# The second block's attention: GpSimd's large operations to VectorE, keys unpadded in pairs, scores in one pool of banks

## The chip, the cores and the metric

The kernel runs on one core of a Trainium2 chip. The metric is the device time of one execution in microseconds (us); lower is better. TensorE multiplies matrices into PSUM, VectorE, ScalarE and GpSimd work elementwise, and the queue of SyncE issues the loads.

## What is computed

Two transformer blocks over 256 tokens of width 1024, in float32. The first (two layers of retention, sliding-window and latent attention with a mixture of experts) is untouched. The second is a hybrid mixer, a projection with residual, and an MLP:

```python
proj = h @ w_in                                   # q, k, v, xl, gl: 512 columns each
q = rms_norm_2(q per head, q_norm_g); k = rms_norm_2(k per head, k_norm_g)
attn = stick_breaking_attention(q, k, v)          # 8 heads of 64
lru = rg_lru(causal_depthwise_conv(xl)) * gelu(gl)
x = x + concatenate([attn, lru]) @ w_out
x = x + square(relu(rms_norm_2(x) @ w_up)) @ w_down
```

and for each head of the attention, with z = q k^T / 8 and the mask kpos < qpos:

```python
log_one_minus = where(mask, log_sigmoid(-z), 0)
suffix = reverse_cumsum(log_one_minus) - log_one_minus
w = where(mask, exp(log_sigmoid(z) + suffix), 0);  out = w @ v
```

## The kernel before

Weights come from HBM in units of 128x1024 float32 (512 KB) into tiles `u`, in the order of use, as many ahead as there are buffers. Each unit is split into two float32r parts: a high half, which ScalarE casts (`unit_hi`, L247), and a low half, the unit minus its high half (`unit_lo`, L251, one subtract of 1024 columns). Every product of a weight is then three matmuls (`mm3`, L377 to L379: high by high, high by low, low by high). `both_halves` makes both parts of a unit ahead of its use on an engine that it names; `unit` does so where that has not happened.

The changed part is `mix_second`. Its first half stands in a block of manual order, so there ScalarE, VectorE and GpSimd run their instructions as they are written: k's RMS scaling (`Normed`: the sums of squares `sums`, the power -0.5 on GpSimd in `roots` and `rpow` at L365, the scaling `apply` at L1471, the transposes `turn` at L1477), the gates and the scan of the recurrent branch (L1535), then the same for q, with the low halves of the q and gl units between. GpSimd makes the low halves of gl units 1 and 3. After that, in `gelu` and in the loop over heads, a list scheduler orders the instructions; `high_priority` puts the heads' steps first.

Keys are laid out twice (`kz`): in one tile the even heads with zeros in the upper 64 rows, in the other the odd heads with zeros in the lower 64, so that each score product contracts 128 rows. For each head, `head` (L1565 on) makes the transposed scores z of 384 columns (the 256 queries against the first 128 keys, and the last 128 queries against the last 128 keys; L1569 and L1570), adds the mask by a product with the identity (L1571, L1572), and forms softplus(z) as max(z, 0) + ln(1 + exp(-|z|)): Abs, Exp and Ln on ScalarE (L1574, L1576, L1577), max and add on VectorE (L1578). `head_w` subtracts the running sums by triangular products into the same bank (L1582 to L1584) and takes the exponential (L1586). `weighted_v` multiplies the weights of two heads with the values, one into the lower and one into the upper 64 partitions (L487, L489), and splits the result. Heads run two ahead of their weights (`DEEP = 2`). The scores of even heads lie in banks of the pool psA, of odd heads in psB (`ZB = "AB"`); each pool has four banks, and psB also takes the results of `weighted_v` and the transposes. psA takes the projections' accumulators too: gl's two, and the four of the output projection.

`gelu` (called at head 1) makes the gate of the recurrent branch: a product on GpSimd (L1550), three operations of 1024 columns on VectorE (L1551 to L1553), Exp, Ln, Exp on ScalarE, and the product L1559 in two halves. The output projection `out_proj` needs four accumulators in psA; its units 0 to 3 take the recurrent branch, 4 to 7 the heads. The low halves of its units 0, 2, 4 and 6 are GpSimd's:

```python
POOL_LO = {("wo", 2): (0, 2, 4, 6)}
ZB = "AB"
```

Of the kernel before, what the change touches and what calls it, by code (L numbers as in the profile page):

```python
# [19 lines left out]
P = 128  # L20
S = 256
# [10 lines left out]
NU, NV, NH = 29, 20, 8  # L32
POOL_LO = {("wo", 2): (0, 2, 4, 6)}
HP = 100
DEEP = 2
ZB = "AB"
TAIL = 5
# [77 lines left out]
def tile_hybrid(ctx: ExitStack, tc: tile.TileContext, A, out, taps=None):  # L115
# [137 lines left out]
    def unit(name):  # L253

        if name not in ready:
            unit_hi(name)
            unit_lo(name, POOL if name[0] in POOL_LO and name[1] in POOL_LO[name[0]] else DVE)
        _, hi, lo = ready.pop(name)
        return [(hi[:, j, :], lo[:, j, :]) for j in range(hi.shape[1])]
# [187 lines left out]

    BLK = (slice(0, 128), slice(128, 384))

    def softmax_p(s, scale, sink):  # L450
# [943 lines left out]
    def mix_second(hT, params, scale, vp):  # L1394
# [50 lines left out]
        qT = st([P, 4, S], F32, "v")  # L1445
        kz = [st([P, 4, S], F32, "v") for _ in range(2)]
        POOL.memset(kz[0][64:128], 0.0)
        POOL.memset(kz[1][0:64], 0.0)

        class Normed:  # L1450
# [12 lines left out]
            def roots(self, i):  # L1463
                s8 = self.s8[i]
                POOL.tensor_scalar(s8[:, 1], s8[:, 0], scale[i][:, 3:4], RMS_EPS, op0=OP.mult, op1=OP.add)
                rpow(s8[:, 2], s8[:, 1])
                POOL.tensor_scalar(s8[:, 2], s8[:, 2], scale[i][:, 2:3], None, op0=OP.mult)

            def apply(self, i):
                self.qn[i] = qn = st([P, 512], F32, "h")  # L1470
                DVE.tensor_tensor(qn.rearrange("p (h e) -> p h e", h=8), self.ps[i].rearrange("p (h e) -> p h e", h=8),  # L1471
                                  self.s8[i][:, 2, :, None].to_broadcast([P, 8, 64]), op=OP.mult)

            def turn(self, i):
                ps = bank("B")
                for b in range(4):
                    PE.transpose(ps[:, b * P:(b + 1) * P], self.qn[i][:, b * P:(b + 1) * P], ident)  # L1477
                pb = ps.rearrange("p (b t) -> p b t", b=4)
                t = slice(i * P, (i + 1) * P)
                if self.name == "q":  # L1480
                    ACT.activation(qT[:, :, t], pb, AF.Copy, scale=qg[:, 0:1])
                else:
                    for b in range(2):
                        r = slice(64 * b, 64 * b + 64)
                        DVE.tensor_scalar(kz[b][r, :, t], pb[r], qg[r, 1:2], None, op0=OP.mult)

# [8 lines left out]
        with tc.manual_schedule(engines={ACT.engine, DVE.engine, POOL.engine}):  # L1495
# [21 lines left out]
            def turn_k(u):  # L1517
                if u == 3:
                    kk.turn(0)
                    both_halves("gl", 0, DVE)  # L1520
                    kk.turn(1)
                    both_halves("gl", 1, POOL)

# [12 lines left out]
            for i in range(2):  # L1536
                qq.apply(i)
            both_halves("gl", 3, POOL)

# [7 lines left out]
        def gelu():  # L1547

            ge = st([P, 4, S], F32, "v")
            POOL.tensor_tensor(u_, u_, gx, op=OP.mult)  # L1550
            DVE.scalar_tensor_tensor(ge, gx, 0.044715, gx, op0=OP.mult, op1=OP.mult)  # L1551
            DVE.scalar_tensor_tensor(ge, ge, 1.0, gx, op0=OP.add, op1=OP.mult)
            DVE.tensor_scalar(ge, ge, -27.0, None, op0=OP.max)  # L1553
            with tc.issue_after(both.ins):
                ACT.activation(ge, ge, AF.Exp, scale=-2.0 * math.sqrt(2.0 / math.pi))
            ACT.activation(ge, ge, AF.Ln, bias=1.0)
            ACT.activation(ge, ge, AF.Exp, scale=-1.0)
            for c in (slice(0, 2), slice(2, 4)):
                DVE.tensor_tensor(aa[:, c], ge[:, c], u_[:, c], op=OP.mult)  # L1559
                split_out(mt[1][0][:, c], mt[1][1][:, c], aa[:, c])  # L1560
            tap("lru", [m[0].bitcast(F32) for m in mix[4:8]])
# [3 lines left out]

        def head(h):
            f, kk = h // 2, kz[h % 2][:, h // 2, :]
            z = bank(ZB[h % len(ZB)])
            PE.matmul(z[:, 0:S], kk[:, 0:P], qT[:, f, :], start=True, stop=False, **kw)  # L1569
            PE.matmul(z[:, S:384], kk[:, P:S], qT[:, f, P:S], start=False, stop=False, **kw)  # L1570
            PE.matmul(z[:, 0:P], identB, masks["m_stick"], start=False, stop=False, **kw)  # L1571
            PE.matmul(z[:, S:384], identB, masks["m_stick"], start=False, stop=True, **kw)  # L1572
            ab = st([P, 384], F32, "h")
            ACT.activation(ab, z[:, :384], AF.Abs)  # L1574
            with tc.issue_after(both.ins):
                ACT.activation(ab, ab, AF.Exp, scale=-1.0)  # L1576
            ACT.activation(ab, ab, AF.Ln, bias=1.0)  # L1577
            DVE.scalar_tensor_tensor(ab, z[:, :384], 0.0, ab, op0=OP.max, op1=OP.add)  # L1578
            return z, ab
# [8 lines left out]

        zs, ws = [], []
        for n in range(8 + DEEP):  # L1590
            if n < 8:
                with tc.high_priority(HP):
                    zs.append(head(n))
            if n == GELU:
# [169 lines left out]
```

## Time and profile before

| | us |
|---|---|
| median of three runs | 808.78 (807.9 to 810.78) |
| the profiled execution, its own time | 816.43 |
| its span, first to last instruction | 814.6 |
| TensorE busy | 776.5 (95%) |
| VectorE busy | 460.0 (56%) |
| ScalarE busy | 337.6 (41%) |
| GpSimd busy | 137.9 (17%) |

The page's shares are means over the whole kernel. The second block's heads and gelu lie between about 577 and 607 us, the output projection from 607 to 630, the MLP from 630 to the end. "PEclk" is the clock granted to TensorE as a share of full speed (2.4 GHz; a half is 1.2). In a timeline, the brackets behind a row give how long the engine had been idle before it and which instruction let it go on. Consecutive rows of one engine can overlap: a record ends when the result is written, and the next instruction starts earlier.

### The profile page before, as it was taken

What the parts mean: (1) busy time and instruction counts of PE and PEld (TensorE: products, weight loads), DVE (VectorE), ACT (ScalarE), POOL (GpSimd) and SP (SyncE); (2) the same over time, 40 slices, a digit from 0 to 9 for tenths busy, and PEclk for the clock granted to TensorE, in tenths of its full rate; (3) what the DMA queues carried; (4) which work ended last, traced back from release to release, by engine and by line L of the source; (5) the groups of instructions that cost most, each with busy time, mean ns of one, the idle gap of its engine ahead of it and who ended that gap; (6) DMA issues with size and microseconds to landing.
All of it is one profiled execution on the core that took longest, in us unless ns stands there. A gap on an engine that the chain in (4) does not pass through costs nothing. (4 is left out here: it accounts for less than half of the span.)

```text
span 814.6 us, 13248 instructions
## 1 busy us (share of the span) xinstructions
PE 776.5 (95%) x5098; PEld 556.8 (68%) x5098; DVE 460.0 (56%) x834; ACT 337.6 (41%) x611; POOL 137.9 (17%) x176
## 2 busy tenths in 40 slices
PE   6999899999999999999899998899879999999998
PEld 4997678443324897778443333598758999999997
DVE  4697745632227688855723216677856655555722
ACT  4566522321213566631311113438764644544710
POOL 1400222260002310102236002114910000000000
PEclk9999999999999999999999999999999999999999
DMA  8992097899999763086899999664403565666101
GB/s 315 407 355 82 1 361 296 304 403 364 411 353 342 280 216 130 27 330 231 306 357 385 407 354 384 213 201 133 139 40 125 185 202 186 199 187 186 50 1 51
DMA packets 57666, 193.45 MB, mean 237 GB/s; under 512 B 8960, under 2 KB 9856, under 8 KB 57600
## 3 DMA queue, kind: packets, MB, share of 16 engines
q1 hardware_dynamic: 57600, 192.57, 65.0%
q8 instruction: 41, 0.67, 0.3%
q14 instruction: 25, 0.20, 0.1%
HBM read 191.50 MB, written 1.05 MB: 236 GB/s over the span
## 5 line engine op out<-in xcount | busy, mean ns | idle before, releaser
L251 DVE TENSOR_TENSOR u<-u,u 128x1024 fp32r<-128x1024 f32 (+5 forms) x151 | 180.6, 1212 | 67.8 <-ACT u L247 41.7
L247 ACT CAST u<-u 128x1024 fp32r<-128x1024 f32 (+4 forms) x159 | 158.1, 1015 | 93.6 <-DVE u L251 44.5
L377 PE MATMUL psA<-u,v 128*128 128x512 f32 (+1 forms) x272 | 111.1, 409 | 6.0 <-ACT u L247 6.0
L1019 PE MATMUL psB<-u,v 128*32 128x512 f32 x864 | 113.9, 602 | 1.9 <-PEq L1143 1.2
L378 PE MATMUL psA<-u,v 128*128 128x512 f32 (+1 forms) x272 | 107.9, 397 | 0.8 <-DVE u L251 0.8
L379 PE MATMUL psA<-u,v 128*128 128x512 f32 (+1 forms) x272 | 107.3, 395 | 0.0
L379 PE MATMUL psB<-v,u 128*128 128x256 f32 x256 | 72.4, 283 | 0.0
L378 PE MATMUL psB<-v,u 128*128 128x256 f32 x256 | 72.3, 283 | 0.0
L377 PE MATMUL psB<-v,u 128*128 128x256 f32 x256 | 72.3, 284 | 0.0
L1019 PEld LDWEIGHTS psB<-u,v 128*32 128x32 f32 x864 | 29.7, 111 | 61.0 <-issue 54.5
L377 PEld LDWEIGHTS psA<-u,v 128*128 128x128 f32 x272 | 52.8, 194 | 16.4 <-ACT u L247 6.5
L1079 PE MATMUL psB<-u,h 128*32 128x512 f32 x496 | 62.7, 594 | 0.8 <-DMA u<-in_exp_w_down_dram 0.8
L378 PEld LDWEIGHTS psA<-u,v 128*128 128x128 f32 x272 | 52.5, 193 | 11.8 <-issue 1.7
L379 PEld LDWEIGHTS psA<-u,v 128*128 128x128 f32 x272 | 52.8, 194 | 10.4 <-issue 0.8
L369 DVE TENSOR_TENSOR h<-psB,h 128x512 fp32r<-128x512 f32 x30 | 20.8, 692 | 59.0 <-ACT h L368 59.0
L377 PE MATMUL psA<-u,h 128*128 128x512 f32 (+1 forms) x136 | 53.0, 390 | 0.0
L378 PE MATMUL psA<-u,h 128*128 128x512 f32 (+1 forms) x136 | 52.7, 387 | 0.0
L379 PE MATMUL psA<-u,h 128*128 128x512 f32 (+1 forms) x136 | 52.0, 386 | 0.0
L378 PEld LDWEIGHTS psB<-v,u 128*128 128x128 f32 x256 | 49.1, 192 | 0.5
L377 PEld LDWEIGHTS psB<-v,u 128*128 128x128 f32 x256 | 48.9, 192 | 0.7 <-ACT v L368 0.2
L379 PEld LDWEIGHTS psB<-v,u 128*128 128x128 f32 x256 | 49.1, 192 | 0.0
L379 PE MATMUL psA<-v,u 128*128 128x256 f32 (+1 forms) x170 | 48.0, 283 | 0.7 <-POOL u L251 0.7
(345 smaller groups left out, 1327.5 us busy)
## 6 DMA issues: line engine op xcount, KB each, us to landing
u<-in_exp_w_gate_up_dram SPq DMA_DIRECT2D x108, 512.0 KB, 6.9
u<-in_exp_w_down_dram SPq DMA_DIRECT2D x62, 512.0 KB, 8.0
u<-in_w_up_dram SPq DMA_DIRECT2D x32, 512.0 KB, 4.4
u<-in_w_down_dram SPq DMA_DIRECT2D x32, 512.0 KB, 3.7
u<-in_w_in_c_dram SPq DMA_DIRECT2D x31, 512.0 KB, 8.1
u<-in_w_out_dram SPq DMA_DIRECT2D x24, 512.0 KB, 5.4
v<-in_exp_w_gate_up_dram SPq DMA_DIRECT2D x20, 512.0 KB, 10.5
v<-in_ln_g_dram SPq DMA_DIRECT2D x4, 512.0 KB, 10.1
```

Source lines behind the costliest of these rows:

```text
L247: return ACT.copy(hi, raw)
L251: return eng.tensor_tensor(lo, raw, hi.bitcast(F32), op=OP.subtract)
L369: DVE.tensor_tensor(dst_lo, src, dst_hi.bitcast(F32), op=OP.subtract)
L377: PE.matmul(ps, ah, bh, start=first, stop=False, **kw)
L378: PE.matmul(ps, ah, bl, start=False, stop=False, **kw)
L379: PE.matmul(ps, al, bh, start=False, stop=last, **kw)
L1019: PE.matmul(hp[32 * e:32 * e + 32, :], XG[k // 2][:, k % 2, i, c:c + CAP], w[e][:, k % 2, :], start=k == 0, stop=k == KD - 1)
L1079: PE.matmul(yp[32 * e:32 * e + 32, :], aT[:, k, 32 * e:32 * e + 32], w[e][:, k, :], start=k == 0, stop=k == 1)
```

## The change

In the second block, GpSimd keeps only the powers of -0.5. The low halves of gl units 1 and 3 and of projection units 0, 2, 4 and 6 are made by VectorE; so is gelu's first product. gelu runs in two halves of 512 columns, each through to its split. In `roots` the scale and the epsilon are added on VectorE, and the last factor moves into `apply`. The keys lie once (`kT`); `pair` makes the scores of two heads, whose 64 rows lie next to each other, by products that contract 64 rows, both in banks of psB. Odd heads form softplus as max(z, ln(1 + exp(min(z, 27)))), with the minimum and the maximum on VectorE; even heads stay as they were.

```diff
-POOL_LO = {("wo", 2): (0, 2, 4, 6)}
-ZB = "AB"
+TOP = 27.0
-            unit_lo(name, POOL if name[0] in POOL_LO and name[1] in POOL_LO[name[0]] else DVE)
+            unit_lo(name, DVE)
+    ROWS = (slice(0, 64), slice(64, 128))
...
-        kz = [st([P, 4, S], F32, "v") for _ in range(2)]
-        POOL.memset(kz[0][64:128], 0.0)
-        POOL.memset(kz[1][0:64], 0.0)
+        kT = st([P, 4, S], F32, "v")
...
-                POOL.tensor_scalar(s8[:, 1], s8[:, 0], scale[i][:, 3:4], RMS_EPS, op0=OP.mult, op1=OP.add)
+                DVE.tensor_scalar(s8[:, 1], s8[:, 0], scale[i][:, 3:4], RMS_EPS, op0=OP.mult, op1=OP.add)
                 rpow(s8[:, 2], s8[:, 1])
-                POOL.tensor_scalar(s8[:, 2], s8[:, 2], scale[i][:, 2:3], None, op0=OP.mult)
...
-                DVE.tensor_tensor(qn.rearrange("p (h e) -> p h e", h=8), self.ps[i].rearrange("p (h e) -> p h e", h=8),
-                                  self.s8[i][:, 2, :, None].to_broadcast([P, 8, 64]), op=OP.mult)
+                DVE.scalar_tensor_tensor(qn.rearrange("p (h e) -> p h e", h=8), self.ps[i].rearrange("p (h e) -> p h e", h=8),
+                                         scale[i][:, 2:3], self.s8[i][:, 2, :, None].to_broadcast([P, 8, 64]),
+                                         op0=OP.mult, op1=OP.mult)
...
-                    for b in range(2):
-                        r = slice(64 * b, 64 * b + 64)
-                        DVE.tensor_scalar(kz[b][r, :, t], pb[r], qg[r, 1:2], None, op0=OP.mult)
+                    DVE.tensor_scalar(kT[:, :, t], pb, qg[:, 1:2], None, op0=OP.mult)
...
-                    both_halves("gl", 1, POOL)
+                    both_halves("gl", 1, DVE)
...
-            both_halves("gl", 3, POOL)
+            both_halves("gl", 3, DVE)
...
-            POOL.tensor_tensor(u_, u_, gx, op=OP.mult)
-            DVE.scalar_tensor_tensor(ge, gx, 0.044715, gx, op0=OP.mult, op1=OP.mult)
...
             for c in (slice(0, 2), slice(2, 4)):
-                DVE.tensor_tensor(aa[:, c], ge[:, c], u_[:, c], op=OP.mult)
+                gc, xc = ge[:, c], gx[:, c]
+                DVE.scalar_tensor_tensor(gc, xc, 0.044715, xc, op0=OP.mult, op1=OP.mult)
+                DVE.scalar_tensor_tensor(gc, gc, 1.0, xc, op0=OP.add, op1=OP.mult)
+                DVE.tensor_scalar(gc, gc, -27.0, None, op0=OP.max)
+                with tc.issue_after(both.ins):
+                    ACT.activation(gc, gc, AF.Exp, scale=-2.0 * math.sqrt(2.0 / math.pi))
+                ACT.activation(gc, gc, AF.Ln, bias=1.0)
+                ACT.activation(gc, gc, AF.Exp, scale=-1.0)
+                DVE.tensor_tensor(u_[:, c], u_[:, c], xc, op=OP.mult)
+                DVE.tensor_tensor(aa[:, c], gc, u_[:, c], op=OP.mult)
                 split_out(mt[1][0][:, c], mt[1][1][:, c], aa[:, c])
...
-        def head(h):
-            f, kk = h // 2, kz[h % 2][:, h // 2, :]
-            z = bank(ZB[h % len(ZB)])
...
+        def pair(f):
+
+            zz = [bank("B") for _ in ROWS]
+            for z, r in zip(zz, ROWS):
+                PE.matmul(z[:, 0:S], kT[r, f, 0:P], qT[r, f, :], start=True, stop=False, **kw)
+            for z, r in zip(zz, ROWS):
+                PE.matmul(z[:, S:384], kT[r, f, P:S], qT[r, f, P:S], start=False, stop=False, **kw)
...
+        def head(z, n):
...
+            if n % 2:
+                DVE.tensor_scalar(ab, z[:, :384], TOP, None, op0=OP.min)
+            else:
+                ACT.activation(ab, z[:, :384], AF.Abs)
             with tc.issue_after(both.ins):
-                ACT.activation(ab, ab, AF.Exp, scale=-1.0)
+                ACT.activation(ab, ab, AF.Exp, scale=1.0 if n % 2 else -1.0)
             ACT.activation(ab, ab, AF.Ln, bias=1.0)
-            DVE.scalar_tensor_tensor(ab, z[:, :384], 0.0, ab, op0=OP.max, op1=OP.add)
+            if n % 2:
+                DVE.tensor_tensor(ab, z[:, :384], ab, op=OP.max)
+            else:
+                DVE.scalar_tensor_tensor(ab, z[:, :384], 0.0, ab, op0=OP.max, op1=OP.add)
...
+                    if n % 2 == 0:
+                        zz = pair(n // 2)
+                    zs.append(head(zz[n % 2], n))
```

The instructions of each engine as the built programs hold them follow; numbers tell buffers apart. In the changed kernel's code L250 is the low half, L376 to L378 are `mm3`, L1468 is `apply`, L1567 and L1569 the score products, L1580, L1587 and L1589 VectorE's steps of a head, L1593 to L1595 the triangular products.

VectorE, from the scaling of q's two halves to the first heads, before (L251 here are projection units 1 and 3; L1413 scales gl's accumulators by token):

```order
L1471 TENSOR_TENSOR h_5856<-psA_5754,s_s_1322_5830 128x512
L1471 TENSOR_TENSOR h_5858<-psA_5755,s_s_1323_5831 128x512
L251 TENSOR_TENSOR u_6176<-u_5601,u_6175 128x1024
L251 TENSOR_TENSOR u_6212<-u_5637,u_6211 128x1024
L1413 TENSOR_TENSOR v_5681<-psA_5866,h_5453 128x512
L1578 SCALAR_TENSOR_TENSOR h_5984<-psA_5979,h_5984 128x384
L1578 SCALAR_TENSOR_TENSOR h_5994<-psB_5989,h_5994 128x384
```

and now (L250: gl unit 3, then projection units 0, 1 and 2):

```order
L1468 SCALAR_TENSOR_TENSOR h_5847<-psA_5749,rms_s_5033,s_s_1321_5823 128x512
L1468 SCALAR_TENSOR_TENSOR h_5849<-psA_5750,rms_s_5034,s_s_1322_5824 128x512
L250 TENSOR_TENSOR u_5854<-u_5408,u_5853 128x1024
L250 TENSOR_TENSOR u_6156<-u_5529,u_6155 128x1024
L250 TENSOR_TENSOR u_6174<-u_5598,u_6173 128x1024
L1580 TENSOR_SCALAR h_5985<-psB_5971 128x384
L250 TENSOR_TENSOR u_6192<-u_5616,u_6191 128x1024
L1589 SCALAR_TENSOR_TENSOR h_5980<-psB_5970,h_5980 128x384
L1587 TENSOR_TENSOR h_5985<-psB_5971,h_5985 128x384
```

Four subtracts stand now ahead of the first head's step, where two stood and two others ran on GpSimd.

TensorE, where the fifth head starts (psA_6050, now psB_6048), before:

```order
L1569 MATMUL psA_6050<-v_5594,v_5595 128x256
L1570 MATMUL psA_6050<-v_5594,v_5595 128x128
L1582 MATMUL psA_5979<-h_5984,cst 128x256
L1582 MATMUL psB_5989<-h_5994,cst 128x256
L1583 MATMUL psA_5979<-h_5984,nones 128x128
L1583 MATMUL psB_5989<-h_5994,nones 128x128
```

and now (psB_6041 takes the first value product):

```order
L1595 MATMUL psB_5970<-h_5980,cst 128x128
L1595 MATMUL psB_5971<-h_5985,cst 128x128
L377 MATMUL psA_5858<-v_5028,u_5853 128x256
L378 MATMUL psA_5858<-v_5027,u_5854 128x256
L487 MATMUL psB_6041<-h_6029,v_5450 64x256
L1567 MATMUL psB_6048<-v_5594,v_5595 128x256
```

The fifth head's scores stood ahead of the first pair's triangular products; they now follow them and the first value product.

TensorE at the end of the heads, before (u_6157 and u_6158 are the halves of projection unit 0):

```order
L1584 MATMUL psA_6087<-h_6092,cst 128x128
L1584 MATMUL psB_6102<-h_6107,cst 128x128
L487 MATMUL psB_6134<-h_6127,v_5450 64x256
L487 MATMUL psB_6134<-h_6132,v_5450 64x256
L489 MATMUL psB_6134<-h_6127,v_5450 64x128
L489 MATMUL psB_6134<-h_6132,v_5450 64x128
L377 MATMUL psA_6151<-u_6157,v_5677 128x512
L378 MATMUL psA_6151<-u_6158,v_5677 128x512
```

and now, from projection unit 0 to the last pair's scores (psB_6085 and psB_6086):

```order
L376 MATMUL psA_6151<-u_6155,v_5674 128x512
L377 MATMUL psA_6151<-u_6156,v_5674 128x512
L378 MATMUL psA_6151<-u_6155,v_5675 128x512
L376 MATMUL psA_6152<-u_6155,v_5674 128x512
L377 MATMUL psA_6152<-u_6156,v_5674 128x512
L378 MATMUL psA_6152<-u_6155,v_5675 128x512
L376 MATMUL psA_6149<-u_6173,v_5674 128x512
L377 MATMUL psA_6149<-u_6174,v_5674 128x512
L1567 MATMUL psB_6085<-v_5594,v_5595 128x256
L1567 MATMUL psB_6086<-v_5594,v_5595 128x256
L1569 MATMUL psB_6085<-v_5594,v_5595 128x128
L1569 MATMUL psB_6086<-v_5594,v_5595 128x128
```

The projection followed the last value product; it now starts ahead of the last pair's scores, with 14 products of its first two units before them, and goes on between the last pair's steps.

## Rows read from the trace of the kernel before

**Rows 1.** Stretches: length, then busy us PE, PEld, DVE, ACT, POOL; clock; DMA.

```profile
573.00:607.00 34.00, 26.61 (x177) 21.72 (x175) 23.31 (x22) 23.27 (x44) 20.16 (x9) 0.95 0.28 92
583.00:591.00 8.00, 7.14 (x48) 5.81 (x46) 7.70 (x7) 6.89 (x15) 8.00 (x4) 1.00 0.67 233
...
596.00:600.00 4.00, 4.00 (x17) 3.04 (x16) 0.56 (x1) 2.69 (x7) 0.00 (x0) 0.57 0.00 0
607.00:814.60 207.60, 203.88 (x1266) 183.82 (x1264) 112.83 (x121) 90.61 (x109) 0.52 (x2) 1.00 0.43 135
```

**Rows 2.** Timeline of TensorE: start, length, engine, line, operation, [idle before <- releaser].

```profile
576.24 0.66 PE L1477 MATMUL psB<-cst,h 128*128 128x128 f32 x4 [0.98 <-DVE h L1471]
...
577.82 0.38 PE L379 MATMUL psA<-v,u 128*128 128x256 f32 x1 [0.70 <-POOL u L251]
...
588.35 0.70 PE L1582 MATMUL psA<-h,cst 128*128 128x256 f32 x2 [0.79 <-DVE h L1578]
...
594.95 0.70 PE L1582 MATMUL psB<-h,cst 128*128 128x256 f32 x2 [3.12 <-DVE h L1578]
...
601.77 0.65 PE L487 MATMUL psB<-h,v 128*64 128x256 f32 x4 [0.22 <-ACT h L1586]
602.25 0.39 PE L489 MATMUL psB<-h,v 128*64 128x128 f32 x4
...
606.19 0.65 PE L487 MATMUL psB<-h,v 128*64 128x256 f32 x4 [1.39 <-ACT h L1586]
...
606.99 0.50 PE L377 MATMUL psA<-u,v 128*128 128x512 f32 x1
```

**Rows 3.** Timeline of VectorE, from the last gate units to gelu.

```profile
569.75 1.22 DVE L251 TENSOR_TENSOR u<-u,u 128x1024 fp32r<-128x1024 f32 x1
...
575.49 0.69 DVE L1471 TENSOR_TENSOR h<-psA,s_s 128x512 f32<-128x512 f32 x1 [1.45 <-POOL s_s L1467]
576.09 6.07 DVE L251 TENSOR_TENSOR u<-u,u 128x1024 fp32r<-128x1024 f32 x2
...
585.52 2.30 DVE L251 TENSOR_TENSOR u<-u,u 128x1024 fp32r<-128x1024 f32 x1
587.75 0.54 DVE L1578 SCALAR_TENSOR_TENSOR h<-psA,h 128x384 f32<-128x384 f32 x1
588.22 2.91 DVE L1551 SCALAR_TENSOR_TENSOR v<-v 128x1024 f32<-128x1024 f32 x1
591.16 3.26 DVE L1552 SCALAR_TENSOR_TENSOR v<-v,v 128x1024 f32<-128x1024 f32 x1
```

**Rows 4.** Timeline of GpSimd over the same time.

```profile
569.46 1.66 POOL L365 TENSOR_TENSOR s_s<-s_s,mhalf 128x8 f32<-128x8 f32 x1
...
575.41 11.33 POOL L251 TENSOR_TENSOR u<-u,u 128x1024 fp32r<-128x1024 f32 x4
586.70 3.35 POOL L1550 TENSOR_TENSOR v<-v,v 128x1024 f32<-128x1024 f32 x1
590.01 3.33 POOL L251 TENSOR_TENSOR u<-u,u 128x1024 fp32r<-128x1024 f32 x1
```

**Rows 5.** Timeline of ScalarE among the first heads.

```profile
581.67 0.94 ACT L1576 ACTIVATE h<-h 128x384 f32<-128x384 f32 x2
...
584.45 1.04 ACT L247 CAST u<-u 128x1024 fp32r<-128x1024 f32 x1 [0.63 <-POOL u L251]
```

**Rows 6.** Timeline of TensorE at the first pair's scores and behind the second's.

```profile
579.24 0.60 PE L1569 MATMUL psA<-v,v 128*128 128x256 f32 x2
...
580.11 0.38 PE L1570 MATMUL psA<-v,v 128*128 128x128 f32 x2
...
582.33 0.36 PE L378 MATMUL psA<-v,u 128*128 128x256 f32 x1
582.53 0.28 PE L379 MATMUL psA<-v,u 128*128 128x256 f32 x1
582.65 0.28 PE L377 MATMUL psA<-v,u 128*128 128x256 f32 x1
```

More of the change, by code (lines that the diff above doesn't have):

```diff
@@ L1549, in gelu @@
             ge = st([P, 4, S], F32, "v")
-            POOL.tensor_tensor(u_, u_, gx, op=OP.mult)
-            DVE.scalar_tensor_tensor(ge, gx, 0.044715, gx, op0=OP.mult, op1=OP.mult)
[L1552 to L1557, printed above, removed]
-            for c in (slice(0, 2), slice(2, 4)):
-                DVE.tensor_tensor(aa[:, c], ge[:, c], u_[:, c], op=OP.mult)
+            for c in (slice(0, 2), slice(2, 4)):
+                gc, xc = ge[:, c], gx[:, c]
[8 more added lines that the diff above has]
+                DVE.tensor_tensor(aa[:, c], gc, u_[:, c], op=OP.mult)
                 split_out(mt[1][0][:, c], mt[1][1][:, c], aa[:, c])
@@ L1564, in mix_second @@
         kw = dict(skip_group_check=True)
-        def head(h):
-            f, kk = h // 2, kz[h % 2][:, h // 2, :]
-            z = bank(ZB[h % len(ZB)])
[L1569 to L1572, printed above, removed]
+        def pair(f):
[4 more added lines that the diff above has]
+                PE.matmul(z[:, S:384], kT[r, f, P:S], qT[r, f, P:S], start=False, stop=False, **kw)
+            for z in zz:
+                PE.matmul(z[:, 0:P], identB, masks["m_stick"], start=False, stop=False, **kw)
+                PE.matmul(z[:, S:384], identB, masks["m_stick"], start=False, stop=True, **kw)
+            return zz
+        def head(z, n):
             ab = st([P, 384], F32, "h")
-            ACT.activation(ab, z[:, :384], AF.Abs)
+            if n % 2:
+                DVE.tensor_scalar(ab, z[:, :384], TOP, None, op0=OP.min)
+            else:
+                ACT.activation(ab, z[:, :384], AF.Abs)
             with tc.issue_after(both.ins):
-                ACT.activation(ab, ab, AF.Exp, scale=-1.0)
+                ACT.activation(ab, ab, AF.Exp, scale=1.0 if n % 2 else -1.0)
             ACT.activation(ab, ab, AF.Ln, bias=1.0)
-            DVE.scalar_tensor_tensor(ab, z[:, :384], 0.0, ab, op0=OP.max, op1=OP.add)
+            if n % 2:
+                DVE.tensor_tensor(ab, z[:, :384], ab, op=OP.max)
+            else:
+                DVE.scalar_tensor_tensor(ab, z[:, :384], 0.0, ab, op0=OP.max, op1=OP.add)
             return z, ab
@@ L1587, in head_w @@
             return wT
-        zs, ws = [], []
+        zs, ws, zz = [], [], []
         for n in range(8 + DEEP):
@@ L1592, in mix_second @@
                 with tc.high_priority(HP):
-                    zs.append(head(n))
+                    if n % 2 == 0:
+                        zz = pair(n // 2)
+                    zs.append(head(zz[n % 2], n))
             if n == GELU:
```

## The prediction

> **What bounds the kernel now.** I read the busy time by stretch first [rows 1]. From 607 us to the end TensorE is busy for 203.88 of 207.60 us at full clock, with DMA at 0.43: whatever ends the second block's attention earlier ends the kernel earlier by as much. In the attention itself, 573 to 607, TensorE is busy for 26.61 of 34.00 us, so 7.39 us are idle; from 596 to 600 it is busy throughout, but the granted clock is 0.57 of full, which costs 4 x 0.43 = 1.7 us. Removable here without taking any product away: **7.4 + 1.7 = 9.1 us**.
>
> Next the TensorE timeline, for whom it waits [rows 2]: 0.98 for the scaling of q, 0.70 for a low half made by GpSimd, 0.79 and 3.12 for VectorE's step of a head (L1578), 0.22 and 1.39 for the last exponentials. These are 7.20 of the 7.39. The projection's first product starts at 606.99, after all eight heads.
>
> Then why VectorE is late. In its timeline [rows 3] a low half takes 1.22 undisturbed, but 6.07 for two, 2.30, 2.91 and 3.26 where GpSimd works beside it: 14.54 against 5 x 1.22 = 6.10, so 8.4 us lost. L1578, which reads PSUM, takes 0.54 in the same place and loses nothing. GpSimd's timeline [rows 4] shows the other side: 11.33 + 3.35 + 3.33 = 18.0 us without a break from 575.41. The two meet on ScalarE, whose cast at 584.45 waited for GpSimd [rows 5]; VectorE's subtract at 585.52 needs that cast, the two gelu steps stand behind it in VectorE's queue, and behind them the L1578 for which TensorE waits its 3.12.
>
> **The change part by part.** *Six low halves and one product leave GpSimd.* VectorE gains 6 x 1.22 plus the product in two halves (2 x 0.69, the row of 512 columns [rows 3]), 8.7 us, and gets back the 8.4. Its sum stays; what goes is an 18 us chain that everything queued behind. Queued behind the new subtracts on VectorE are the heads' steps, each up to 1.2 us later. The order printed above has four subtracts between the scaling of q and the first head's step, where two stand now. The last of them ends near 576 + 3 x 1.2 = 580, about when ScalarE has the first head ready, so they cost little; at the old 3 us each they would cost about 7.
>
> *The scaling of q.* GpSimd keeps only the power (1.66 us [rows 4]); its three queued small steps per half become one on VectorE. The trace has no such step of 8 columns on VectorE; its price lies between 0 and 0.54 (384 columns [rows 3]), and I take 0.15, near the lower end for so few columns. L1471 waited 1.45 us for GpSimd [rows 3]; now the scan alone precedes it. The first 0.98 goes, and the 0.70 with it: the last gate unit's low half ends about 1.2 us after the scaling, while TensorE still has eight products without it to do.
>
> Here a rule bears. Beside the remaining power of 1.66 us, which reads two SBUF operands, a low half on VectorE took its undisturbed 1.22 [rows 3, 4]; so I charge nothing. The Trainium skill, "SBUF — State Buffer", "Who interferes with whom", says that a VectorE instruction with two SBUF inputs and a GpSimd one that reads SBUF exclude each other for a whole instruction; by that the two powers of q could hold VectorE for 2 x 1.66 = 3.3 us, and the time would be 804.8. The low halves beside the large operations agree with the page, this row does not.
>
> *Keys unpadded.* One scaling instead of two, two memsets less: TensorE does not wait for either now, worth 0. The heads' first products now contract 64 rows, two heads next to each other on different rows. Today two of 256 columns take 580.11 - 579.24 = 0.87 us [rows 6], two of 128 half of that: 1.31 a pair, 5.2 for four pairs. No 64-row product is in the trace. One bound is that two run side by side as the value products on 64 columns do: four records, two products, start to start 0.48 (to 602.25) instead of 0.87 [rows 2], 0.55 of the time, so 4 x 0.59 = 2.4 us less (2.6 if free of loss). The other is that they run one after the other and pay for changing the shape: at each change from one kind of product to another a product takes 0.20 start to start instead of 0.12 [rows 6], and if the array also has to empty, the 0.16 between a record's 0.28 and its 0.12 step: 8 x 0.16 = 1.3 more. I take 2.2 less: the 64-column row is the same case turned by a quarter, and 0.2 is kept for waits that reappear. The Trainium skill, "TensorEngine Tiling (Array Packing)", "Key Properties", says both things: tiles run in parallel, and a change of tiling mode drains the engine. By the first the sum is as I have it, by the second alone 3.5 worse; no row shows 64 rows.
>
> *Banks.* All heads' scores lie in the four banks of psB, beside the value products. The four of psA are free for the projection, so its products, the first half of which needs only the recurrent branch, can be issued among the last two heads: the order above shows 14 of them ahead of the last pair's keys. That fills the waits of 3.12 and 1.39, or what is left of them. The price is the fifth head's: its keys now wait for the bank of an earlier head.
>
> *Odd heads and gelu.* Four Abs leave ScalarE (0.47 each, as an Exp of that size [rows 5]) and four minima of 0.54 enter VectorE; gelu runs in halves, so the projection's first two units can start after half of it.
>
> **What waits stay.** Laying the printed order on these durations, I get: about 0.7 for the first value product (its exponential stands on ScalarE behind a cast of 1.04 [rows 5]), 0.5 for the fifth head's bank, 0.5 for the second value product, 0.8 for the sixth head's step behind gelu on VectorE: 2.5. With VectorE a tenth slower throughout it is 4.5. I take 3.0. The projection among the heads adds some twelve changes of kind at 0.08, 1.0 us.
>
> **Sum:** 9.1 - 3.0 - 1.0 + 2.2 = **7.3 us**. The profiled execution took 816.43 us (span 814.6); the median without a profile is 808.78, 7.65 less. The stretch is engine time and not profiling, so I carry the 7.3 over: **801.5 us**, and 809.1 in a profile.
>
> **Rivals.**
> *Pairs do not run side by side* (part of the change does not do what it says): 5.1 with no drain, 3.8 with it: 803.7 to 805. For: no 64-row product in the trace. Against: the 64-column row.
> *Banks hold the heads back.* Only two pairs fit psB, and a value product takes a bank as well. If each of the three later starts costs 1 us more than I took, the gain is 4.3: 804.5. For: the fifth head now stands behind the first value product in the order. Against: today's waits of this kind come from VectorE, none from a bank.
> *The powers hold VectorE.* If both of q's stop the instruction beside them for 1.66 us each, the scaling of q and all behind it come 3.3 later: 804.8. For: GpSimd's large operations do this. Against: the row at 569.75.
> *The clock falls in the head stage and the kernel is slower.* Between 583 and 597 I have TensorE busy for about 11.5 of 14 us in short pieces. At half clock these take 23 us, 9 more than the stretch has: 7.3 - 9 = -1.7, 810.5. It decides once more than about 85% of this work runs (11.5 x 0.85 less the 2.5 of waits it fills is 7.3) at 1.2 GHz. Against it: at 7.14 busy of 8.00 with gaps up to 0.79 the clock stayed at 1.00, and it fell only after the wait of 3.12 [rows 1, 2]; my largest gap is 0.8.
> *The low halves stay long*, because something other than GpSimd stretched them: the first four cost about 7 us and the gain is gone, 808 to 809. Against: they follow GpSimd's activity, and the one at 569.75, beside a power of eight columns only, is at 1.22 [rows 3, 4].
>
> **How the numbers follow.** Chances: the forecast, 798 to 803.5, 0.50; pairs not side by side 0.18; banks 0.14; powers 0.04; low halves long or otherwise no difference 0.08; clock 0.06. Best end: all waits but 1.5 gone, 0.5 for changes, 2.6 from the pairs: 9.7, so 799; I give it 1 us more. Upper end: waits of 4.5 to 5, changes 1.5, no gain from pairs and half the drain: 2.0 to 2.5, 806.5. Range 798 to 806.5. A measurement of this kernel tells about 0.3% (2.4 us) from no change: faster by more 0.86, within 0.08, slower 0.06, from the same cases.
>
> **What would show it.** VectorE's low halves at 1.22 throughout, no GpSimd instruction over 2 us after 565; the second turn of q near 575.3; pair products at about 0.5 for two; projection products from about 593 on between the heads; TensorE idle about 3 us from 573 to 607, clock 1.00 throughout; the last projection product near 622.5 instead of 629.6. The forecast is wrong if a wait over 2 us is left among the heads, if the clock falls, or if the stretch after the projection shows new waits for weights.

## The result, and the profile after

The changed kernel takes **801.26 us** (median of 4 runs, 799.69 to 802.6; the kernel before beside it 809.78): ratio 0.9885, interval 0.9851 to 0.9919. Forecast were 801.5 and 798 to 806.5. Twelve more runs on another chip gave 803.56 against 808.71, ratio 0.9941 (0.9916 to 0.9966). So the change gains 5 to 9 us, and the first median lay at the good end.

The traces tell the gain more closely. They differ only in one stretch: from the first product of the gate projection to the transposes behind the output projection's last product. TensorE's timeline of the kernel before has these ends (start, length, engine, line, operation, count):

```profile
566.02 0.28 PE L377 MATMUL psA<-v,u 128*128 128x256 f32 x1
...
629.84 0.38 PE L1616 MATMUL psB<-cst,v 128*128 128x128 f32 x2
```

and that of the changed kernel, with the waits between in brackets:

```profile
557.81 0.28 PE L376 MATMUL psA<-v,u 128*128 128x256 f32 x1
...
576.05 0.65 PE L487 MATMUL psB<-h,v 128*64 128x256 f32 x2 [0.62 <-ACT h L1597]
...
583.77 0.70 PE L1593 MATMUL psB<-h,cst 128*128 128x256 f32 x2 [0.30 <-DVE h L1589]
...
585.77 0.70 PE L1593 MATMUL psB<-h,cst 128*128 128x256 f32 x2 [0.50 <-DVE h L1587]
...
586.67 0.48 PE L376 MATMUL psA<-u,v 128*128 128x512 f32 x1
...
615.73 0.49 PE L1629 MATMUL psB<-cst,v 128*128 128x128 f32 x3
```

The stretch is 629.84 - 566.02 = 63.82 us before and 57.92 after: **5.9 us less**. Behind it both kernels take the same, 814.6 - 629.84 = 184.76 and 800.5 - 615.73 = 184.77; in all fourteen traces of this study it is 184.8 to 185.0. The part ahead of it, whose order on TensorE is the same in both, took 566.02 in the one and 557.81 in the other; over the fourteen traces it runs from 555.8 to 566.0, without regard to the stretch. So most of the scatter of the profiled times is made there, and of the 14.1 us by which the two spans differ 8.2 are not the change's.

The waits of [rows 2], 7.20 us, are now 1.42. The stretches' rows (length, busy us of PE, PEld, DVE, ACT, POOL, granted clock, DMA share, GB/s), which answer to [rows 1]:

```profile
573.00:593.00 20.00, 18.30 (x101) 13.02 (x100) 18.10 (x30) 17.37 (x33) 0.00 (x0) 1.00 0.27 88
593.00:599.00 6.00, 6.00 (x33) 4.53 (x32) 4.13 (x6) 3.55 (x8) 0.00 (x0) 1.00 0.30 90
607.00:800.50 193.50, 189.76 (x1203) 172.14 (x1202) 103.85 (x110) 83.81 (x99) 0.51 (x2) 1.00 0.44 137
```

GpSimd does nothing, and the clock stays at 1.00 where it had fallen to 0.57. VectorE's timeline, beside [rows 3]: three low halves in 3.71 where two took 6.07, and gelu's operations on half the columns at 0.68 where the whole ones took 2.91 and 3.26.

```profile
565.65 1.38 DVE L1468 SCALAR_TENSOR_TENSOR h<-psA,rms_s,s_s 128x512 f32<-128x512 f32 x2
566.96 3.71 DVE L250 TENSOR_TENSOR u<-u,u 128x1024 fp32r<-128x1024 f32 x3
...
577.01 0.68 DVE L1548 SCALAR_TENSOR_TENSOR v<-v 128x512 f32<-128x512 f32 x1
```

### The profile page after: what moved, and what is told of

Its sections match the earlier page's. It is cut to its first block, busy times and chain, and to the rows that moved or that the text cites. A ratio compares the mean times of both kernels' runs of the same rounds, so it can differ in the third digit from the quotient of the medians.

```text
span 800.5 us, 13228 instructions
## 1 busy us (share of the span) xinstructions
PE 771.2 (96%) x5098; PEld 550.7 (69%) x5098; DVE 460.4 (58%) x851; ACT 336.6 (42%) x610; POOL 110.0 (14%) x159
## 5 line engine op out<-in xcount | busy, mean ns | idle before, releaser
L250 DVE TENSOR_TENSOR u<-u,u 128x1024 fp32r<-128x1024 f32 (+5 forms) x157 | 183.1, 1181 | 71.6 <-ACT u L246 44.3
L376 PE MATMUL psA<-u,v 128*128 128x512 f32 (+1 forms) x272 | 110.5, 406 | 5.4 <-ACT u L246 5.4
L378 PE MATMUL psA<-u,v 128*128 128x512 f32 (+1 forms) x272 | 106.1, 391 | 0.0
L378 PE MATMUL psB<-v,u 128*128 128x256 f32 x256 | 72.4, 283 | 0.0
L376 PE MATMUL psB<-v,u 128*128 128x256 f32 x256 | 72.3, 284 | 0.0
L376 PEld LDWEIGHTS psA<-u,v 128*128 128x128 f32 x272 | 52.1, 192 | 15.1 <-ACT u L246 5.4
L377 PEld LDWEIGHTS psA<-u,v 128*128 128x128 f32 x272 | 52.2, 192 | 12.1 <-DVE u L250 1.9
L378 PEld LDWEIGHTS psA<-u,v 128*128 128x128 f32 x272 | 52.0, 191 | 10.4 <-issue 1.2
L376 PE MATMUL psA<-u,h 128*128 128x512 f32 (+1 forms) x136 | 53.0, 389 | 0.0
L378 PE MATMUL psA<-u,h 128*128 128x512 f32 (+1 forms) x136 | 52.0, 386 | 0.0
L376 PEld LDWEIGHTS psB<-v,u 128*128 128x128 f32 x256 | 48.9, 192 | 0.8 <-ACT v L367 0.2
L378 PEld LDWEIGHTS psB<-v,u 128*128 128x128 f32 x256 | 49.1, 192 | 0.0
L376 PE MATMUL psA<-v,u 128*128 128x256 f32 (+1 forms) x170 | 48.3, 285 | 0.0
```

Source lines behind the costliest of these rows:

```text
L250: return eng.tensor_tensor(lo, raw, hi.bitcast(F32), op=OP.subtract)
L376: PE.matmul(ps, ah, bh, start=first, stop=False, **kw)
L377: PE.matmul(ps, ah, bl, start=False, stop=False, **kw)
L378: PE.matmul(ps, al, bh, start=False, stop=last, **kw)
```

## The experiments

All are the changed kernel with one thing undone, unless said otherwise. The first four expectations count the stretch from VectorE's scan (58.96 before, 52.44 after). Since GpSimd lengthens the scan itself, as a run below shows, I compare by the stretch defined above. "Waits" are those of TensorE inside it, "lowest clock" the lowest granted clock of a 4 us slice in it.

| | ratio to before, interval | stretch | waits | lowest clock |
|---|---|---|---|---|
| before | 1 | 63.8 | 7.2 | 0.57 |
| changed, first | 0.9885 (0.9851 to 0.9919) | 57.9 | 1.4 | 1.00 |
| changed, again | 0.9941 (0.9916 to 0.9966) | 57.9 | 1.4 | 1.00 |
| before + move alone | 0.9953 (0.9933 to 0.9972) | 60.6 | 4.3 | 0.70 |
| before + move + small steps | 0.9967 (0.9941 to 0.9993) | 61.0 | 3.6 | 0.66 |
| move undone | 1.0003 (0.9981 to 1.0026) | 64.7 | 6.4 | 0.50 |
| only the projection's low halves back on GpSimd | 0.9973 (0.9948 to 0.9998) | 60.9 | 3.6 | 1.00 |
| small steps undone | 0.9972 (0.9944 to 1.0) | 59.9 | 1.9 | 1.00 |
| gelu whole | 1.0024 (1.0 to 1.0047) | 64.7 | 6.1 | 0.51 |
| gelu whole, banks of two pools | 0.9979 (0.9952 to 1.0007) | 62.6 | 4.8 | 0.50 |
| banks of two pools | 0.9927 (0.9898 to 0.9956) | 57.9 | 0.7 | 1.00 |
| third pair in psA | 0.9952 (0.9924 to 0.9981) | 58.1 | 2.3 | 0.58 |
| keys padded | 0.9928 (0.9903 to 0.9953) | 58.5 | 2.1 | 1.00 |
| all heads by Abs | 0.9938 (0.9915 to 0.9962) | 58.4 | 1.8 | 1.00 |

The changed kernel beside the others:

> The changed kernel itself, beside the next three on the same chip: the time that their differences are taken from. 801.3 as before, ratio to the kernel before 0.9885 or up to 0.991; the stretch from the gate projection's first product to the transposes behind the output projection's last product 57.9 us, as in its first trace (63.8 before).

Measured 803.56 us; the ratio misses 0.991, the stretch is 57.92 again, with the same three waits.

### The move

On the kernel before:

```diff
-POOL_LO = {("wo", 2): (0, 2, 4, 6)}
+POOL_LO = {}
-                    both_halves("gl", 1, POOL)
+                    both_halves("gl", 1, DVE)
-            both_halves("gl", 3, POOL)
+            both_halves("gl", 3, DVE)
-            POOL.tensor_tensor(u_, u_, gx, op=OP.mult)
+            DVE.tensor_tensor(u_, u_, gx, op=OP.mult)
```

> The kernel before with one part of the change alone: the six low halves and gelu's first product (whole, 1024 columns) on VectorE; padded keys, banks of two pools, whole gelu and GpSimd's small steps stay. 'The stretch' is the time from the scan of the recurrent branch to the transposes behind the projection's last product, 58.96 us in the trace of before and 52.44 in that of after. Theory (GpSimd's large operations held VectorE up, and that was most of the loss): low halves at 1.22, no wait over 2 us, clock 1.00, stretch about 54.5, time about 5 us under before, 804.5. Rival 1 (unpadded keys and row pairs bring most): stretch 57.5, 807.5 or more. Rival 2 (the banks, which let the projection run among the heads, bring most): TensorE still waits for the last heads, stretch 57, 807.

Measured 805.67 us, and from the scan 54.58: the theory's stretch. But the clock did fall, and TensorE's timeline keeps waits for the scaling of q, for the last heads and for gelu's split ahead of the projection:

```profile
569.85 0.66 PE L1477 MATMUL psB<-cst,h 128*128 128x128 f32 x4 [1.49 <-DVE h L1471]
...
592.23 0.65 PE L487 MATMUL psB<-h,v 128*64 128x256 f32 x4 [0.91 <-ACT h L1586]
...
594.63 0.52 PE L377 MATMUL psA<-u,v 128*128 128x512 f32 x1 [1.53 <-ACT v L368]
```

The reverse, the move undone in the changed kernel (`POOL_LO` back, gl 1 and 3 and gelu's product, in halves, on GpSimd):

> The changed kernel with only the move undone: low halves of gl units 1 and 3 and of projection units 0, 2, 4 and 6, and gelu's first product (in halves) on GpSimd again. Theory: low halves of VectorE beside them take over 2 us again, a wait of over 2 us among the heads is back, stretch 57 to 58, time 806 to 807. Rival 1 or 2 (the rest brings most): stretch at most 54, time at most 803.

Measured 808.45 us, from the scan 59.60: the whole gain is gone, more than the theory asked. VectorE's timeline has the long operations again:

```profile
573.84 2.78 DVE L251 TENSOR_TENSOR u<-u,u 128x1024 fp32r<-128x1024 f32 x1 [0.52 <-issue]
...
583.61 3.57 DVE L1549 SCALAR_TENSOR_TENSOR v<-v 128x512 f32<-128x512 f32 x2
```

Then only the four low halves of the projection, back on GpSimd:

> The changed kernel with only the low halves of projection units 0, 2, 4 and 6 back on GpSimd; gl's and gelu's product stay on VectorE. Theory (any large operation of GpSimd holds the VectorE instruction beside it, and VectorE's queue holds the heads): three of the four fall on the heads' first steps, each costs VectorE about 2 us, a wait of over 1.5 us is back, stretch 61, time 806. Rival (only gl's low halves, which TensorE needs for the gates and the heads wait behind, mattered): stretch 58, 803.5.

Measured 808.81 us, stretch 60.9: the size was right, the way was not. Three of the four cost VectorE something: a half of gelu took 1.65, a step of gelu's split 2.49, and the scan grew, 4.58 for four where the changed kernel has 2.44 (VectorE, then GpSimd, then TensorE's wait behind it):

```profile
571.40 4.58 DVE L1532 TENSOR_TENSOR_SCAN v<-v,v 128x256 f32<-128x256 f32 x4
```

```profile
572.94 2.48 POOL L251 TENSOR_TENSOR u<-u,u 128x1024 fp32r<-128x1024 f32 x1
```

```profile
576.67 1.31 PE L1476 MATMUL psB<-cst,h 128*128 128x128 f32 x8 [1.99 <-DVE h L1469]
```

### The small steps

```diff
-                DVE.tensor_scalar(s8[:, 1], s8[:, 0], scale[i][:, 3:4], RMS_EPS, op0=OP.mult, op1=OP.add)
+                POOL.tensor_scalar(s8[:, 1], s8[:, 0], scale[i][:, 3:4], RMS_EPS, op0=OP.mult, op1=OP.add)
                 rpow(s8[:, 2], s8[:, 1])
+                POOL.tensor_scalar(s8[:, 2], s8[:, 2], scale[i][:, 2:3], None, op0=OP.mult)
```

with `apply` as before.

> The changed kernel with q's and k's small steps around the power on GpSimd again and the two-operand scaling. Theory: the waits of TensorE for the scaling of q that the run with the move alone shows (0.39 and 1.49) are back: stretch 59.6, 1.7 more in time. Rival (the scaling of q is hidden behind the gate's products): stretch 57.9, no difference.

Measured 806.11 us, stretch 59.9: the theory's size, but not by its waits alone. Waits of 1.09 and 0.24 for the scaling and the last low half return and put TensorE 1.3 us behind:

```profile
569.80 0.66 PE L1475 MATMUL psB<-cst,h 128*128 128x128 f32 x4 [1.09 <-DVE h L1469]
```

Half a us of that is taken back, since gate products are put off into the wait for the first value product, which goes. All waits together are 1.85 instead of 1.42, only 0.4 more. The other 1.6 of the 2.0 is work of TensorE, whose instructions stand in another order from the second value product on; what in that order costs so much is not shown. GpSimd's timeline tells why the scaling is late: beside VectorE its steps of 8 columns take 1.18, 0.96 and 1.03, the last, undisturbed, 0.31.

```profile
561.75 1.18 POOL L1463 TENSOR_SCALAR s_s<-s_s,rms_s 128x8 f32<-128x8 f32 x1 [11.59 <-DVE s_s L1459]
563.02 1.66 POOL L364 TENSOR_TENSOR s_s<-s_s,mhalf 128x8 f32<-128x8 f32 x1
564.77 0.96 POOL L1465 TENSOR_SCALAR s_s<-s_s,rms_s 128x8 f32<-128x8 f32 x1
565.83 1.03 POOL L1463 TENSOR_SCALAR s_s<-s_s,rms_s 128x8 f32<-128x8 f32 x1
...
568.71 0.31 POOL L1465 TENSOR_SCALAR s_s<-s_s,rms_s 128x8 f32<-128x8 f32 x1
```

Was GpSimd then the whole story? The kernel before with the move and the small steps:

> The kernel before with two parts of the change: the large operations on VectorE, and the small steps around the power too; padded keys, banks of two pools, whole gelu, Abs for all heads stay. Theory (GpSimd is the whole story): the waits of 0.39 and 1.49 for the scaling of q, which the run with the move alone shows, go: stretch 60.6 - 1.9 = 58.7, time 803.5 to 804, the same as the changed kernel within the measurement. Rival (halves, banks, pairs or odd heads are worth 2 us or more by themselves): stretch 60, time 805.5.

Measured 806.3 us, stretch 61.0: the rival. Waits of 0.98 and 1.59 for the last heads and gelu's split stay, and the clock falls to 0.66 behind them. The wait for the scaling of q is down from 0.39 and 1.49 to 0.48, and yet the stretch is no shorter than with the move alone (60.6). More is needed.

### gelu and the banks

```diff
-            for c in (slice(0, 2), slice(2, 4)):
-                gc, xc = ge[:, c], gx[:, c]
-                DVE.scalar_tensor_tensor(gc, xc, 0.044715, xc, op0=OP.mult, op1=OP.mult)
+            DVE.tensor_tensor(u_, u_, gx, op=OP.mult)
+            DVE.scalar_tensor_tensor(ge, gx, 0.044715, gx, op0=OP.mult, op1=OP.mult)
...
+            for c in (slice(0, 2), slice(2, 4)):
+                DVE.tensor_tensor(aa[:, c], ge[:, c], u_[:, c], op=OP.mult)
```

> The changed kernel with gelu's operations whole again (1024 columns, all on VectorE and ScalarE, only the last product and the split in halves). Theory (with GpSimd out of the way VectorE has room, and the halves only shorten what stands ahead of a head's step and let the projection start half a gelu earlier): the projection's first products come about 2 us later and a wait of 0.5 to 1 us is back: stretch 58.7, 0.8 more in time, not to be told from none. Rival (the halves are what makes the projection run among the heads): stretch 60, 2 to 2.5 more.

Measured 810.79 us, stretch 64.7: far beyond both. TensorE's timeline has one wait for it, the longest of the study, and the slices around it show the price:

```profile
597.91 0.80 PE L376 MATMUL psA<-u,v 128*128 128x512 f32 x1 [5.13 <-ACT v L367]
```

```profile
592.00:596.00 4.00, 0.78 (x6) 0.56 (x4) 2.45 (x3) 3.63 (x4) 0.00 (x0) 1.00 0.41 134
596.00:600.00 4.00, 2.09 (x6) 1.21 (x6) 3.25 (x6) 2.25 (x5) 0.00 (x0) 0.63 0.32 128
600.00:604.00 4.00, 4.00 (x18) 2.76 (x20) 0.56 (x1) 2.06 (x6) 0.00 (x0) 0.51 0.00 0
```

The product waits for gelu's split, and the last pair's scores stand behind it in TensorE's queue (they start at 599.92). So the halves and the banks may be one thing: do the halves matter only because the projection is let in early? Both undone (the lines above, and in `pair`: `bank(p) for p in "AB"`):

> The changed kernel with both the banks and gelu's halves undone (even heads' scores in psA, gelu whole). With only gelu whole TensorE stood 5.13 us at the projection's first product, which lay in its queue ahead of the last pair's scores; here the projection lies behind all heads. Theory (the halves are needed only because the banks let the projection in ahead of the last pair): no wait over 1.5 us, clock at 1.00 in the head stage, stretch 58 to 59, time 4 to 6 us under before, 803 to 804.5. Rival (whole operations of gelu hold up the heads by themselves): a wait of over 2 us, stretch 61 or more, 806.5 or more.

Measured 808.27 us, stretch 62.6: the rival's numbers. The scores no longer stand behind the projection, and the waits for the heads are only 0.72 and 0.74. But gelu itself is late, and TensorE has nothing else to do:

```profile
592.86 0.79 PE L376 MATMUL psA<-u,v 128*128 128x512 f32 x1 [3.33 <-ACT v L367]
```

Counted from the stretch's start the projection begins at 41.0 us before, at 36.1, 36.5, 37.1 and 33.9 in the four other kernels with whole gelu, and at 27.8 to 33.2 in those with halves (36.1 with the move undone). In those four a wait ahead of the projection ends with gelu's split; the halves let TensorE leave the heads earlier, as long as GpSimd does not delay them. The banks alone, `zz = [bank(p) for p in "AB"]`:

> The changed kernel with only the banks undone: of each pair the even head's scores lie in psA, the odd head's in psB, so the projection's accumulators in psA come free only with the last even head and 3 of its products instead of 29 stand ahead of the last triangular products. Theory: about 2 us of waits at the last heads come back, stretch 54.5, 803.5. Rival 2 (banks bring most): 5 us come back, stretch 57.5, 806.5. Rival 3 (four banks for all heads hold the fifth and sixth head back by as much as the overlap gains): no difference, stretch 52.4, 801.3.

Measured 804.07 us, from the scan 52.40: rival 3's result, no difference. The projection starts 3.5 us later (32.4). TensorE waits only 0.72 us instead of 1.42 in all, and its own work is longer by as much; whether the want of banks is what holds the changed kernel's heads back, as the rival has it, is not shown.

```profile
594.68 0.50 PE L376 MATMUL psA<-u,v 128*128 128x512 f32 x1 [0.72 <-ACT v L367]
```

### Keys, pairs and odd heads

Padded keys, in the same order of products (the two tiles, their memsets and the second scaling on VectorE are back too):

```diff
-                PE.matmul(z[:, 0:S], kT[r, f, 0:P], qT[r, f, :], start=True, stop=False, **kw)
+                PE.matmul(z[:, 0:S], kk[:, f, 0:P], qT[:, f, :], start=True, stop=False, **kw)
```

> The changed kernel with only the keys padded again: two tiles with 64 rows of zeros, score products of 128 rows, written in the same order. Theory: a pair that stands together takes 1.31 us instead of 0.85 start to start, three pairs do so, the fifth and sixth head stand apart and change nothing; one more scaling on VectorE is hidden: 1.4 more, stretch 53.8, 802.7. The prediction's term as it was written: 2.2 more, 803.5. Rival 1 (keys and pairs bring most): 5 more, 806. Rival 4 (TensorE's waits for the other engines take the gain up): no difference, 801.3.

Measured 803.51 us; from the scan 52.00, by the stretch 58.5. That is 0.6 more, and the waits alone grew by 0.7. TensorE's own work is 58.51 - 2.10 = 56.4 with padded keys and 57.92 - 1.42 = 56.5 without: rival 4's result, and not for its reason.

Two of the three new waits, 0.25 and 0.49, stand ahead of all scores, and VectorE's second scaling makes them. Laying out half of the keys takes VectorE 1.51 with padded keys, as before, and 0.75 in the changed kernel (VectorE before, VectorE changed, then TensorE with padded keys):

```profile
563.05 1.51 DVE L1485 TENSOR_SCALAR v<-psB,qkg 64x512 f32<-64x512 f32 x2 [0.51 <-PE psB L1477]
```

```profile
554.83 0.75 DVE L1481 TENSOR_SCALAR v<-psB,qkg 128x512 f32<-128x512 f32 x1 [0.51 <-PE psB L1475]
```

```profile
566.03 0.39 PE L378 MATMUL psA<-v,u 128*128 128x256 f32 x1 [0.25 <-DVE u L250]
...
569.17 1.31 PE L1477 MATMUL psB<-cst,h 128*128 128x128 f32 x8 [0.49 <-DVE h L1470]
```

Counted from the stretch's start the scan begins 1.0 us later for it, at 6.5 instead of 5.5. The expectation had the second scaling hidden; it was not.

For the products the order is the same, so the rows can be laid side by side. The changed kernel, two pairs side by side, then the fifth head, which stands alone:

```profile
569.48 0.70 PE L1567 MATMUL psB<-v,v 64*128 64x256 f32 x4
570.01 0.39 PE L1569 MATMUL psB<-v,v 64*128 64x128 f32 x4
...
571.72 0.36 PE L377 MATMUL psA<-v,u 128*128 128x256 f32 x1
...
576.85 0.70 PE L1567 MATMUL psB<-v,v 64*128 64x256 f32 x2
577.47 0.70 PE L1593 MATMUL psB<-h,cst 128*128 128x256 f32 x2
...
578.32 0.49 PE L1569 MATMUL psB<-v,v 64*128 64x128 f32 x2
578.74 0.49 PE L1595 MATMUL psB<-h,cst 128*128 128x128 f32 x2
579.06 0.22 PE L1571 MATMUL psB<-m_stick,identB 128*128 128x128 bf16 x1
```

and the same with padded keys:

```profile
572.14 1.03 PE L1571 MATMUL psB<-v,v 128*128 128x256 f32 x4
573.00 0.61 PE L1573 MATMUL psB<-v,v 128*128 128x128 f32 x4
...
575.23 0.36 PE L377 MATMUL psA<-v,u 128*128 128x256 f32 x1
...
579.95 0.70 PE L1571 MATMUL psB<-v,v 128*128 128x256 f32 x2
580.48 0.59 PE L1597 MATMUL psB<-h,cst 128*128 128x256 f32 x2
...
581.58 0.22 PE L1575 MATMUL psB<-m_stick,identB 128*128 128x128 bf16 x1
```

A pair's two products of 256 columns take 0.53 instead of 0.86, and two pairs with all around them 571.72 - 569.48 = 2.24 instead of 3.09; with 0.08 more from the last gate product to the first of them, 0.77 less. The last pair saves 0.35 more. But the fifth head takes 579.06 - 576.85 = 2.21 instead of 1.63, and the sixth, by the same count, 2.31 instead of 1.64: a product of 64 rows alone among those of 128 costs about 0.1 us each time the kind changes. 0.77 + 0.35 - 0.58 - 0.67 = **-0.1**: the row pairs give nothing. What unpadded keys bring is the scaling that VectorE is spared.

Could the third pair stand together, in psA (`bank("BBAB"[f])`)?

> The changed kernel with the third pair of heads (the fifth and sixth) in psA instead of psB, so that its two heads need not wait for a bank and can stand side by side. Theory (every pair side by side, two waits for banks less, but 3 of the projection's products instead of 29 ahead of the last triangular products): stretch 57.3, time 0.5 less than the changed kernel, not to be told from none. Rival (the projection behind the last pair leaves its waits bare): stretch 59, time 1 us more.

Measured 806.05 us, stretch 58.1: neither. The wide products of the fifth and sixth head come 0.79 us apart instead of 4.06 (576.85 and 580.91 in the changed kernel), but a mask product stands between them, and each still takes 0.63, as a lone one does:

```profile
571.72 0.70 PE L1567 MATMUL psA<-v,v 64*128 64x256 f32 x2
572.35 0.23 PE L1571 MATMUL psB<-m_stick,identB 128*128 128x128 bf16 x1
572.51 0.70 PE L1567 MATMUL psA<-v,v 64*128 64x256 f32 x2
```

Their narrow products lie 2.4 us apart. So a bank for each head brings the two closer, and the scheduler's order parts them all the same: what a third pair side by side would be worth is not shown. With the projection behind the last pair TensorE waits 2.26 us, and the clock falls:

```profile
588.05 0.70 PE L1593 MATMUL psB<-h,cst 128*128 128x256 f32 x2 [2.26 <-DVE h L1587]
```

```profile
584.00:588.00 4.00, 1.79 (x15) 1.05 (x13) 3.69 (x7) 3.76 (x10) 0.00 (x0) 1.00 0.00 0
588.00:592.00 4.00, 3.94 (x14) 3.15 (x14) 2.89 (x4) 2.97 (x6) 0.00 (x0) 0.58 0.73 262
```

Odd heads as even ones (`if n % 2` always false):

> The changed kernel with odd heads as even ones: Abs on ScalarE, no minimum on VectorE, so ScalarE has 4 x 0.47 = 1.9 us more and VectorE 4 x 0.5 less. Theory: ScalarE was busy for 21.92 of the 27 us from 573 and is what TensorE's longest wait (0.62) ends on, so about 1 of the 1.9 shows: stretch 58.9, 1 more in time. Rival (neither engine bounds the heads any more): stretch 57.9, no difference.

Measured 804.66 us, stretch 58.4: half of what the theory asked, and within the measurement no difference.

## Why the prediction held, step by step

**What bounds the kernel: right.** The head stage waited for VectorE, VectorE for GpSimd. With the move undone the waits, the long low halves and the half clock are back and the gain is zero.

**Removable, 9.1: right**, 8.9 in the stretch (7.2 of waits and 1.7 of clock).

**Low halves at 1.22 and 8.4 back: right.** The first four subtracts cost no head a wait, as said.

**The scaling of q: right in its waits.** The first two waits of [rows 2], 1.68, are gone. With the small steps undone 1.33 of waits come back there; that the stretch grew by 2.0 in all owes more to TensorE's other order than to them. The small step took 0.23 instead of 0.15; q's two turns follow each other from 566.44 on; with the 8.21 us by which the stretch starts earlier in this trace, the second is near 575.2, where 575.3 was forecast.

**The powers hold VectorE (rival): no.** GpSimd's timeline of the changed kernel has the two at

```profile
560.41 4.47 POOL L364 TENSOR_TENSOR s_s<-s_s,mhalf 128x8 f32<-128x8 f32 x2 [13.20 <-DVE s_s L1463]
```

each over 2 us (2.48 and 2.02) instead of 1.66, while VectorE beside them runs a low half at 1.22 and four scans at 2.44. In this trace GpSimd was the slower for it, in the one with the small steps undone neither (1.66 each). The Trainium skill, "SBUF — State Buffer", "Who interferes with whom", has a GpSimd read and a VectorE instruction with two SBUF inputs exclude each other, whoever issues first. The large operations agree (the scans at 4.58); for the two powers no run shows VectorE held.

**Waits left, 3.0: too many**, 1.4. They lie where they were laid, at the first value product (0.62 of 0.7) and at the third pair's weights (0.30 and 0.50), but the fifth head's bank and the second value product cost nothing.

**One scaling instead of two, worth 0: wrong.** With the second scaling back TensorE waits 0.25 and 0.49 ahead of the scores. That the early waits went to nothing is partly its doing.

**Changes of kind, 1.0: too few.** With padded keys, where the score products are as before, TensorE's work is 56.4 against 63.82 - 7.2 - 1.7 = 54.9: 1.5. That is the rest of the account, with idle times too short for a bracket in it, and not a count of changes. With the third pair in psA, where the projection begins 4.3 us later, the work is 58.1 - 2.3 - 1.7 = 54.1 (1.7 for the clock), so it moves by over 2 us with the order; what in the order does it is not shown.

**Row pairs, 2.2: the step that failed.** They do run side by side, 0.53 against the 0.48 taken from the value products, but the term counted four pairs, and only three stand together. The fifth and sixth head's products stand alone in TensorE's order and pay at each change of kind. I had the delay by the bank as a wait and did not see that the order also parts the pair; the run with a bank for each of the two shows that banks are not the whole reason. Measured -0.1. The Trainium skill, "TensorEngine Tiling (Array Packing)", "Key Properties", has both halves of it: tiles in parallel, and a drain at a change of mode. The rows agree with both (0.53 for two; 0.1 at a change), and here they cancel.

**The sum:** 8.9 - 1.4 - 1.5 - 0.1 = 5.9, where 9.1 - 3.0 - 1.0 + 2.2 = 7.3 was forecast. The measured terms add up by construction, since the 1.5 is what the others leave. Waits smaller by 1.6 made up for most of the 2.3 that the pairs lack, which is luck, and so is the first median, 801.26, that fell on the forecast of 801.5. The two measured gains, 8.5 and 5.2, enclose the 5.9 of the stretch; by it the forecast is some 1.5 us too low.

**The profiled time, 809.1: wrong.** It was 802.3. The 7.65 us between the profiled run of before and its median were carried over as the profile's cost; they were the untouched part's scatter.

**Banks: wrong in weight.** Its fill was to take up the waits of 3.12 and 1.39; without it the stretch is the same. The projection started at 28.9 after the stretch's start, 594.9 on the old clock instead of 593. **gelu's halves** got one clause, "the projection's first two units can start after half of it", and no price: undone, they cost 6.8 us, or 4.7 with the banks undone too. They were the second pillar of the gain, and no rival put the projection at the head of TensorE's queue with gelu not yet done.

**The clock: right for the change, near for its neighbours.** It stayed at 1.00, but six of the altered kernels in the table show it fall.

The parts do not add up: 6.8, 6.8 and 2.0 for undoing the move, the halves or the small steps are far more than 5.9. The first two leave TensorE with waits among the heads, and the clock falls with them; the third leaves the clock at 1.00 and makes TensorE's work longer. Added to the move alone, the small steps gave nothing (61.0 after 60.6). The list scheduler made another order of TensorE's instructions for each of the three, so none of these is the price of one part by itself. What stays open: whether padded keys with the rest of the change would be as fast; 58.5 against 57.9 is not told apart by the times.

## What to carry to other kernels

An engine that helps out can cost the engine it relieves more than it saves: look in its timeline for whether the relieved engine's operations have grown. When work is let in early on a queue that runs in order, ask what it needs and what then stands behind it: here cutting the producer in halves paid either way, and letting the consumer in early gave nothing with the halves and made things worse without them. Narrow products pay side by side only where the printed order has them side by side; an isolated one pays at each change of kind.

## What the runs showed of the hardware

- VectorE's scan with two SBUF inputs grows beside a GpSimd subtract of 128x1024: four took 4.58 instead of 2.44, one GpSimd operation of 2.48 beside them.
- GpSimd's steps of 8 columns take 0.96 to 1.18 beside VectorE and 0.31 alone.
- Two products of 64 rows and 256 columns on different rows took 0.53 from the start of the first to the next product, where two of 128 rows took 0.86; one such product alone took 0.62 where one of 128 rows took 0.53.
- The granted clock has two levels here, 1.00 (2.4 GHz) and 0.5 (1.2 GHz). Its mean in a slice of 4 us fell to between 0.50 and 0.70 during or just behind waits of 2.26, 3.12, 3.33 and 5.13 us among the heads, behind 0.91 and 1.53 or 0.98 and 1.59 close together, and, with the move undone, at waits of 1.65 and 0.80. It did not fall behind 1.99 at the scaling of q, where TensorE's products ran gap-free before it, nor behind 1.69 among the heads with the move undone. No run tells these cases apart by a cause.
